# Output projection of a two-layer diffusion block: latent tiles kept in PSUM through both norms, and a planner that knows a shared port

## The chip, the cores and the metric

One core of a Trainium2 chip runs the whole program in one launch. Its engines are TensorE (PE, matmuls; PEld is its weight load), VectorE (DVE), ScalarE (ACT), GpSimd (POOL) and SyncE (SP, which issues most of the DMAs). The metric is the device time of one execution in microseconds, as the median of several runs.

## The reference

Two layers over 1024 latent tokens and 256 context tokens, 1024 channels, everything in float32. Each layer makes modulation vectors, projects the tokens, runs two kinds of attention and a convolution, and joins them in `o`. The part that matters here comes behind that, and then a mixture of 16 experts in which each expert takes its best tokens:

```python
x  = layer_norm(ALPHA * x + g1 * (o @ w_out[l]), ln1_g[l], ln1_b[l])   # ALPHA = sqrt(2)
h2 = layer_norm(x) * (1 + sc2) + sh2
aff = softmax(h2 @ w_router[l])                  # 16 experts
g, idx = top_k(aff.T, 128)                       # 128 latents (32 context tokens) for each expert
x  = layer_norm(ALPHA * x + g2 * scatter_add(experts(h2[idx]) * g), ln2_g[l], ln2_b[l])
```

The context tokens go the same way in layer 0 alone. In layer 1 only the latents do.

## The kernel before

Per layer, `p2` (with `p1`) projects, the attention follows, `p4` (line 1574) does the output projection, the two norms, the router and the search for the experts' tokens, and `moe` runs the experts. A float32 product is made of three matmuls on operands split into a high and a low part (`hi`, `lo`).

`p4` goes by tiles of 128 tokens: eight of latents, and in layer 0 two of context behind them. A tile's steps, with their lines:

1. Load the attention's output `ot` and the reciprocal sums `rb`, multiply them (L1700, on DVE for tiles 0 and 1, else on POOL), take the high part (L1710 on DVE, L1712 on ACT) and the low part (L1715, on DVE for latents, on POOL for context).
2. 48 matmuls in two halves of 512 columns (L1732 to L1734) into PSUM tiles `po` of one bank each; four are in rotation.
3. For latents, DVE multiplies each half by the gate row out of PSUM into an SBUF tile `t1` (L1742), which frees the bank, and adds the residual: `x*ALPHA + t1` (L1836). For context, ACT copies `po` to `t1` and POOL does the rest.
4. Statistics by halves (L1764), aggregation (L1770), epsilon (L1771), and the power -1/2 on POOL (L1774).
5. The first norm with its gain and shift (`lng`, `lnb`), by the tile's kind. Kind "d" (tiles 0 to 3): DVE makes -mean*rstd on one column (L1791), ACT normalizes (L1794), POOL multiplies by the gain (L1818), DVE adds the shift (L1820). Kind "h" (tiles 4 to 6) is the same in halves (L1807, L1810, L1813). Kind "f" (tile 7) is two DVE passes (L1785, L1788).
6. ACT scales the result by ALPHA into `ac` (L1844), which SP stores for the closing of the layer. Statistics again, and the second norm with the modulation rows, in the same kind.
7. SP stores the tile. PE transposes it (L1866), ACT copies that out (L1871), PE makes the logits (L1880), DVE the maximum (L1884), ACT the exponential (L1888), DVE the reciprocal and the division (L1891, L1892). PE transposes the affinities (L1901) and ACT keeps them in `aff` (L1905).

When all the latents' affinities are there, DVE searches: 16 rounds of MAX8, FIND_INDEX8 and MATCH_REPLACE8 (L1987 to L1990). The positions feed an indirect DMA (L2081) that fetches the tokens for `moe`.

The order of the work in `p4` is written by a planner, `Plan`: every operation has an engine, a price in us, operations that it needs, and slots that it takes (`t1=4, po=4, ...`). An engine that comes free takes the ready operation with the longest way to the end, and each engine's queue gets the operations in this order; at run time a queue is strictly in order. The planner knew the engines, not what two of them share:

```python
            return max(t, free.get(o["eng"], 0.0))          # Plan.run: when an operation can start
        ...
        P = Plan(ot=3, rb=3, x=2, oh=3, t1=4, po=4, tp=2, hT=1, lg=2, ac=1, raw=4, w=4)
        ...
    KINDS = [["dd"] * 4 + ["hh"] * 3 + ["ff", "dd", "ff"]] * 2
    GE, TE, LE = "pp", "pp", "pp"
```

The first weights of layer 1's experts are loaded while `p4` runs. Four of them are split there, `w_hi` on ACT (L2044) and `w_lo` on POOL (L2050). They are traced behind the plan, in a block of their own; a split gives its load's place free, and SP then loads another weight into it:

```python
            for c in range(self.PAIRS):
                self.w_hi(c)
                self.w_lo(l, c, nc.gpsimd)
                self.w_load(l, len(ring) + c)
```

Of the kernel before, what the change touches and what calls it, by code (L numbers as in the profile page):

```python
# [8 lines left out]
F32 = mybir.dt.float32  # L9
# [130 lines left out]
# ---------------------------------------------------------------- the kernel  # L140

class Plan:
    """Orders operations by a forecast: each has an engine, a price in us and the operations it needs. An engine that
    comes free takes the ready operation with the longest way to the end. A resource has n slots, taken in turn."""
# [11 lines left out]
    def op(self, eng, cost, f, after=(), new=(), use=(), lag=None, rank=0.0):  # L156
        o = dict(eng=eng, cost=cost, f=f, after=[x for x in after if x], new=list(new), 
                 lag=self.lags.get(eng, self.LAG) if lag is None else lag, own=lag is None or lag <= self.LAG,
                 rank=rank, n=len(self.ops), end=None)
        for h in (*new, *use):  # L160
            h["users"].append(o)
        self.ops.append(o)
        return o

    def run(self):
# [11 lines left out]
        def start(o):  # L177
# [9 lines left out]
            return max(t, free.get(o["eng"], 0.0))  # L187
        while ready:
# [16 lines left out]
class Kern:  # L205
# [5 lines left out]
    # -- small helpers  # L211
# [20 lines left out]
    def place(self, pool, shape, dt, *names):  # L232
        """Fixes the order of a pool's tiles in memory."""
# [6 lines left out]
    def split(self, hi, lo, src, hi_eng="act"):  # L240
        """src = hi + lo, hi of 12 bits."""
# [7 lines left out]
    def bcast_rows(self, src, n, parts=128):  # L249
        """A row of n values in DRAM, as an access pattern that repeats it over partitions."""  # L250
# [9 lines left out]
    # -- constants  # L260
# [96 lines left out]
    def adaln_col(self, w, junk, l, t, i):  # L357
        """Column t of a layer's modulation vectors, for x (0) or the context (1)."""
# [26 lines left out]
    def nrm(self, p, mv, n, tag):  # L385
        """(rstd, -mean * rstd), both [128, n]."""
# [4 lines left out]
    def ln_fast(self, x, mean, rs, g, b):  # L391
        """A norm with its affine map on the vector engine alone."""
# [4 lines left out]
    def ln_a(self, x, rs, nm, g):  # L397
        """A norm and its gain."""
# [4 lines left out]
    def p1(self, l, p, ps, vhi, vlo, W, prep_load, prep_split):  # L403
        """Closes the layer before (l > 0), first norm and modulation, values, the first projections."""
# [15 lines left out]
        # the values' weights  # L420
# [33 lines left out]
        for n, t in enumerate(tiles):  # L454
# [13 lines left out]
            if n == 2 and l > 0:  # L468
                ld.append(P.op("scatter", self.XS, lambda: None, after=ld[-1:]))  # the last scatter
# [88 lines left out]
        # transposed, modulated, in two parts  # L558
# [34 lines left out]
        # values  # L593
# [18 lines left out]
        # gates of the convolution, first tokens  # L612
# [48 lines left out]
    # -- projections  # L661

    def p2(self, l):
# [13 lines left out]
        # the lower part overlaps what the experts hold longest  # L677
# [24 lines left out]
        # the rest, channels on partitions  # L702
# [128 lines left out]
    # -- attention  # L831
# [21 lines left out]
    def early(self, l):  # L853
        """Masks, sinks and room for the first units of attention."""
# [19 lines left out]
    def early_units(self, l):  # L874
        """The row maxima of the first two units, as closures."""
# [9 lines left out]
    def keys(self, p, name, n, src):  # L885
        """Per head [k_hi; k_lo] and [k_hi; 1], keys along the free axis."""
# [25 lines left out]
    def su_load(self, u, srcs, part):  # L912
        """A unit's 1024 query columns: [hi; hi] and [lo; maximum]; srcs gives (columns, hi, lo)."""
# [24 lines left out]
    def su_rows(self, u, sink, dst):  # L938
        """The last row of the queries' second part, the negated maximum, and the sink's weights."""
# [112 lines left out]
    def make_units(self, l):  # L1052
# [4 lines left out]
        # 8 blocks of 128 queries: columns (kv head, head, query)  # L1057
# [22 lines left out]
        # heads over all queries of the grid  # L1080
# [37 lines left out]
        # the context's queries: kv head g, columns (head, query)  # L1118
# [75 lines left out]
    def recip(self, src, outs, w, sink=None):  # L1194
        """outs = 1 / (src + sink), runs of values in DRAM, w to a partition; two stages."""
# [71 lines left out]
    def conv_ln(self, P, l, un, after):  # L1267
        """The norm over a unit's channels, as operations."""
# [49 lines left out]
        # silu(y) = h (1 + tanh h), h = y / 2  # L1318
# [31 lines left out]
    def attention(self, l):  # L1350
# [140 lines left out]
        # the rest of the modulation, the output projection's weights  # L1491
# [18 lines left out]
        # the convolution  # L1510
# [21 lines left out]
        # the reciprocals of the denominators  # L1532
# [28 lines left out]
    # -- output projection, second modulation, routing  # L1561
# [12 lines left out]
    def p4(self, l):  # L1574
# [12 lines left out]
        # affinities: experts on partitions, the halves of the latents from 0 and 32, the context from 64  # L1587
# [916 lines left out]
```

## Time and profile before

| what | value |
|---|---|
| time, median of 3 runs | 2952.28 us (2948.66 to 2956.59) |
| profiled execution, span from first to last instruction | 2951.7 us; no time beside the span is recorded for it |
| PE busy | 2632.2 us, 89% |
| DVE busy | 2228.7 us, 76% |
| ACT busy | 1618.6 us, 55% |
| POOL busy | 949.7 us, 32% |
| mean granted clock of PE | 0.942 of full speed |

Busy time counts from an instruction's start to its end, so what an instruction waits for inside itself counts as busy. The `p4` stages lie at about 600 to 813 us (layer 0) and 2116 to 2315 us (layer 1) from the span's start.

### The profile page before, as it was taken

The page shows a single profiled execution, that of the slowest core. Times are in us where ns is not written, and L with a number is a line of the kernel's source. Part 1 is how long each engine was busy: PE and PEld are TensorE (multiplying, and loading weights), DVE is VectorE, ACT ScalarE, POOL GpSimd, SP SyncE. Part 2 cuts the span into 40 slices and gives each one's busy share as a digit, 9 for nine tenths or more (in the row PEclk, how much of TensorE's full clock was granted, in tenths as well). Part 3 has the DMA queues.
Part 4 walks back from the last instruction along what each step waited for, and adds up shares of the span by engine and source line. Part 5 has one row for each costly group of instructions (what it writes and reads, how often), then busy time and mean ns, then how long its engine had stood idle before and what let it go on. Part 6 is the DMA issues. An engine that isn't in the chain of part 4 may idle for free. (4 is left out here: it accounts for less than half of the span.)

```text
span 2951.7 us, 37404 instructions
## 1 busy us (share of the span) xinstructions
PE 2632.2 (89%) x13657; PEld 2070.0 (70%) x13657; DVE 2228.7 (76%) x3074; ACT 1618.6 (55%) x2045; POOL 949.7 (32%) x680
## 2 busy tenths in 40 slices
PE   7998988988589999999999499999986599999995
PEld 4986544566479898988888388655565477777774
DVE  6367598478869998888887835566588788888888
ACT  3224667623346665666666343687433377777774
POOL 2046687345412120201110516685054011111113
PEclk8999999989689999999999699999996799999998
DMA  6254744483458897979886414563453699999983
GB/s 244 74 181 148 202 136 108 115 245 120 188 211 314 309 335 285 336 292 327 301 319 226 149 54 157 172 184 104 138 183 151 235 372 373 372 374 372 373 341 135
DMA packets 204353, 682.86 MB, mean 231 GB/s; under 512 B 25637, under 2 KB 97630, under 8 KB 148870
## 3 DMA queue, kind: packets, MB, share of 16 engines
q1 hardware_dynamic: 191834, 641.23, 59.9%
q0 software_dynamic: 12336, 39.25, 5.3%
q8 instruction: 107, 1.75, 0.2%
q14 instruction: 76, 0.62, 0.1%
HBM read 600.45 MB, written 79.84 MB: 230 GB/s over the span
## 5 line engine op out<-in xcount | busy, mean ns | idle before, releaser
L2050 DVE TENSOR_TENSOR lo<-raw,hi 128x2048 fp32r<-128x2048 f32 x284 | 641.1, 2284 | 7.2 <-ACT hi L2044 7.1
L2044 ACT ACTIVATE hi<-raw 128x2048 fp32r<-128x2048 f32 x289 | 552.1, 1913 | 86.1 <-PE gu L2164 38.1
L2124 PE MATMUL gu<-xt,hi 128*128 128x320 f32 x2048 | 528.7, 332 | 0.9 <-DVE xt L2110 0.9
L2125 PE MATMUL gu<-xt,lo 128*128 128x192 f32 x2048 | 513.1, 251 | 0.0
L2240 POOL DMA_INDIRECT s_acc<-yo,i x31 | 76.3, 2462 | 1121.2 <-DVE yo L2238 1121.2
L1252 POOL TENSOR_TENSOR cy<-cy,csq 128x512 f32<-128x512 f32 (+1 forms) x300 | 386.1, 1302 | 109.2 <-ACT csq L1248 100.0
L2125 PEld LDWEIGHTS gu<-xt,lo 128*128 128x128 f32 x2048 | 392.4, 192 | 0.6
L2124 PEld LDWEIGHTS gu<-xt,hi 128*128 128x128 f32 x2048 | 385.6, 188 | 1.8 <-DVE xt L2110 1.1
L1178 PE MATMUL O<-P,v 128*65 128x512 f32 (+7 forms) x592 | 279.5, 561 | 12.9 <-ACT P L1171 12.6
L1248 ACT ACTIVATE csq<-ch,cw 128x512 f32<-128x512 f32 (+1 forms) x300 | 198.9, 673 | 46.9 <-POOL cy L1252 43.2
L2163 PE MATMUL gu<-hi,xt 128*128 128x512 f32 x512 | 204.5, 399 | 0.0
L2164 PE MATMUL gu<-hi,xt 128*128 128x512 f32 x512 | 202.8, 396 | 0.0
L2165 PE MATMUL gu<-lo,xt 128*128 128x512 f32 x512 | 202.8, 396 | 0.0
L730 PE MATMUL pj<-hhi,whi 128*128 128x512 f32 (+1 forms) x512 | 188.4, 368 | 9.1 <-ACT whi L244 9.1
L732 PE MATMUL pj<-hhi,wlo 128*128 128x512 f32 (+1 forms) x512 | 188.0, 367 | 1.1 <-DVE wlo L247 1.1
L731 PE MATMUL pj<-hlo,whi 128*128 128x512 f32 (+1 forms) x512 | 187.8, 367 | 0.0
L2050 DVE TENSOR_TENSOR lo<-more,hi 128x2048 fp32r<-128x2048 f32 x80 | 182.1, 2284 | 0.0
L2044 ACT ACTIVATE hi<-more 128x2048 fp32r<-128x2048 f32 x80 | 152.1, 1906 | 19.5 <-PE gu L2206 9.8
L1732 PE MATMUL po<-hi,ohi 128*128 128x512 f32 x288 | 123.0, 427 | 41.1 <-DVE ohi L1710 17.4
L361 DVE CUSTOM_DVE_ANT_0 adj<-adw,srow,bmod 128x1024 bf16<-128x1024 f32 x96 | 133.7, 1392 | 33.3 <-DMA adw<-in_wmt 31.6
L1171 ACT ACTIVATE P<-ST 128x512 f32<-128x512 f32 (+1 forms) x200 | 114.5, 580 | 51.8 <-PE ST L1154 28.2
L2132 ACT ACTIVATE t<-gu 128x320 f32<-128x320 f32 x128 | 55.4, 433 | 119.3 <-PE gu L2125 119.0
(318 smaller groups left out, 6004.2 us busy)
## 6 DMA issues: line engine op xcount, KB each, us to landing
raw<-in_wmoe SPq DMA_DIRECT2D x289, 1024.0 KB
more<-in_wmoe SPq DMA_DIRECT2D x80, 1024.0 KB
adw<-in_wmt SPq DMA_DIRECT2D x24, 1024.0 KB
srow<-in_wmoe SPq DMA_DIRECT2D x15, 1024.0 KB
wraw<-in_win SPq DMA_DIRECT2D x26, 512.0 KB
x<-in_x SPq DMA_DIRECT2D x16, 512.0 KB
adw<-in_wmt SPq DMA_DIRECT2D x16, 512.0 KB
q<-s_q SPq DMA_DIRECT2D x64, 128.0 KB
```

Source lines behind the costliest of these rows:

```text
L730: nc.tensor.matmul(o[:, :w], whi[:, k], hhi[:, k, sl], start=k == 0, stop=False)
L732: nc.tensor.matmul(o[:, :w], wlo[:, k], hhi[:, k, sl], start=False, stop=k == 7)
L1178: nc.tensor.matmul(o[:V1, o0:o0 + w], self.v[:, t["kt"], t["v"] * V1:t["v"] * V1 + V1], t["P"][:, :w], start=t["first"], stop=t["last"] is ...
L1248: nc.scalar.activation(z[:, :w], h, AF.Copy, scale=c)
L1252: nc.gpsimd.tensor_tensor(st["y"], st["y"], st.pop(("z", t))[:, :w], op=ALU.add)
L2044: self.nc.scalar.activation(h, self.S["raw", i], AF.Copy)
L2050: eng.tensor_tensor(lo, r, h.bitcast(F32), op=ALU.subtract)
L2124: nc.tensor.matmul(o[:, f, :320], hi[:, k, fs], xt[:, k], start=k == 0, stop=False)
L2125: nc.tensor.matmul(o[:, f, :192], lo[:, k, fs], xt[:, k, :192], start=False, stop=k == 7)
L2163: nc.tensor.matmul(o, xt[:, kk, 0], hi[:, k], start=kk == 0, stop=False)
L2164: nc.tensor.matmul(o, xt[:, kk, 1], hi[:, k], start=False, stop=False)
L2165: nc.tensor.matmul(o, xt[:, kk, 0], lo[:, k], start=False, stop=kk == 7)
```

## The change

The latents' tiles now stay in PSUM. One `po` tile holds both halves in two banks, and two such tiles are in rotation instead of four halves. Gate, sum, both norms and the statistics work in place on it (new function `affine_o`, two DVE passes per norm); only the second norm's shift writes `t1` in SBUF, in halves. The kinds "d" and "h" are gone for latents, and with them ACT's normalization and POOL's gain products. The low part `lo` of tiles 2 to 7 moves from DVE to POOL. Context tiles keep their way, but for -mean*rstd, which is a `tensor_scalar` now. The softmax division moves from DVE to ACT.

The plan gets a resource "port": every priced POOL operation, and each DVE operation marked with `port=True`, takes it, so that no two of these are planned at once. Several prices are changed. In layer 1, the four weight splits get an order in the queues: `w_hi` behind the last `keep` on ACT, `w_lo` behind the last `root` on POOL.

The diff, cut to its core (comments and docstrings, which the change also takes out, are left out here):

```diff
-    def __init__(self, slack=0.0, lags=None, **slots):
+    def __init__(self, slack=0.0, lags=None, ported=False, **slots):
+        self.ported = ported
...
-    def op(self, eng, cost, f, after=(), new=(), use=(), lag=None, rank=0.0):
+    def op(self, eng, cost, f, after=(), new=(), use=(), lag=None, rank=0.0, port=False):
+        port = self.ported and (port or eng == "pool" and lag is None and cost > 0)
...
-            return max(t, free.get(o["eng"], 0.0))
+            return max(t, free.get(o["eng"], 0.0), free.get("port", 0.0) if o["port"] else 0.0)
...
+            if o["port"]:
+                free["port"] = o["end"]
...
-        P = Plan(ot=3, rb=3, x=2, oh=3, t1=4, po=4, tp=2, hT=1, lg=2, ac=1, raw=4, w=4)
+        P = Plan(ported=True, ot=3, rb=3, x=2, oh=3, t1=4, po=2, tp=2, hT=1, lg=2, ac=1, raw=4, w=4)
...
-            pick = lambda s: po if ctx and s[i - 8] == "p" else ve
-            e, el, et = pick(self.GE), pick(self.LE), pick(self.TE)
+            el, et = po if i > 1 else ve, po if ctx and self.TE[i - 8] == "p" else ve
...
+            hp = P.new("po")
             for n in range(2):
-                hp = P.new("po")
...
-                        if k == 0:
-                            q["o", n] = self.rot(ps, [128, 512], F32, "po", 4)
-                        o, ns = q["o", n], slice(n * 512, n * 512 + 512)
+                        if n == 0 and k == 0:
+                            q["o"] = self.rot(ps, [128, 2, 512], F32, "po", 2)
+                        o, ns = q["o"][:, n], slice(n * 512, n * 512 + 512)
...
-                    o = P.op(pe, 1.29, mm, [parts[k], W[k], o], new=[hp] if k == 0 else [],
-                             use=[H["oh"], hw[k]] + ([hp] if k else []), rank=old)
+                    o = P.op(pe, 1.395, mm, [parts[k], W[k], o or first], new=[hp] if n == 0 and k == 0 else [],
+                             use=[H["oh"], hw[k]] + ([hp] if n or k else []), rank=old)
+                    first = first or o
...
+                def gate(q=q, n=n, cond=cond):
+                    nc.vector.tensor_tensor(q["o"][:, n], q["o"][:, n], rows[cond][0][:, n * 512:n * 512 + 512], op=ALU.mult)
...
+            hold = H["t1"] if ctx else hp
...
-                    nc.vector.bn_stats(q["st"][:, n, :], q["t1"][:, n * 512:n * 512 + 512])
+                    nc.vector.bn_stats(q["st"][:, n, :], q["t1"][:, n * 512:n * 512 + 512] if ctx else q["o"][:, n])
...
-                    nc.gpsimd.tensor_tensor(q["rs"], q["rs"], self.mhalf[:, :1], op=ALU.pow)
+                    ends_at[po] = nc.gpsimd.tensor_tensor(q["rs"], q["rs"], self.mhalf[:, :1], op=ALU.pow)
...
+            def affine_o(dep, g, b, uses, new=None, q=q):
+                two = lambda x: x.rearrange("p (a b) -> p a b", a=2)
+                def f1():
+                    nc.vector.scalar_tensor_tensor(q["o"], q["o"], q["mv"][:, 0, 0:1], two(g()), op0=ALU.subtract, op1=ALU.mult)
+                def f2():
+                    nc.vector.scalar_tensor_tensor(q["o"], q["o"], q["rs"], two(b()), op0=ALU.mult, op1=ALU.add)
+                def f3(n):
+                    if n == 0:
+                        q["t1"] = self.rot(p, [128, D], F32, "t1", 4)
+                    ns = slice(n * 512, n * 512 + 512)
+                    nc.vector.scalar_tensor_tensor(q["t1"][:, ns], q["o"][:, n], q["rs"], b()[:, ns], op0=ALU.mult, op1=ALU.add)
+                u = dict(use=[hp] + uses, rank=old)
+                o = P.op(ve, 1.28, f1, dep, **u)
+                if new is None:
+                    o = P.op(ve, 1.28, f2, [o], **u)
+                    return [o, o]
+                o1 = P.op(ve, 0.7, lambda: f3(0), [o], new=[new], **u)
+                return [o1, P.op(ve, 0.7, lambda: f3(1), [o1], use=u["use"] + [new], rank=old)]
...
-                    nc.vector.scalar_tensor_tensor(q["nm"], q["mv"][:, :, 0], -1.0, q["rs"], op0=ALU.mult, op1=ALU.mult)
+                    nc.vector.tensor_scalar(q["nm"], q["mv"][:, :, 0], q["rs"], -1.0, op0=ALU.mult, op1=ALU.mult)
...
-                        nc.vector.scalar_tensor_tensor(q["t1"][:, ns], q["x"][:, ns], ALPHA, q["t1"][:, ns],
+                        nc.vector.scalar_tensor_tensor(q["o"][:, n], q["x"][:, ns], ALPHA, q["o"][:, n],
                                                        op0=ALU.mult, op1=ALU.add)
...
-            o = affine([o, *ln], kinds[0], lambda: lng, lambda: lnb, [])
+            o = affine([o, *ln], kinds[0], lambda: lng, lambda: lnb, []) if ctx else \
+                affine_o([o, *ln], lambda: lng, lambda: lnb, [])
...
-                nc.scalar.activation(q["ac"], q["t1"], AF.Copy, scale=ALPHA)
+                nc.scalar.activation(q["ac"], q["t1"] if ctx else q["o"].rearrange("p a b -> p (a b)"), AF.Copy, scale=ALPHA)
...
                 nc.vector.reciprocal(q["sm"][:, 2:3], q["sm"][:, 1:2])
-                nc.vector.tensor_scalar(q["e"], q["e"], q["sm"][:, 2:3], None, op0=ALU.mult)
+            def share(q=q):
+                nc.scalar.activation(q["e"], q["e"], AF.Copy, scale=q["sm"][:, 2:3])
...
-                self.w_hi(c)
-                self.w_lo(l, c, nc.gpsimd)
+                with self.tc.issue_after(ends_at[ac].ins):
+                    self.w_hi(c)
+                with self.tc.issue_after(ends_at[po].ins):
+                    self.w_lo(l, c, nc.gpsimd)
...
-    KINDS = [["dd"] * 4 + ["hh"] * 3 + ["ff", "dd", "ff"]] * 2
-    GE, TE, LE = "pp", "pp", "pp"
+    KINDS = "dd", "ff"
+    TE = "pp"
```

## Rows read from the trace of the kernel before

**Rows 1.** Windows by stage: length, busy PE, PEld, DVE, ACT, POOL, clock, DMA.
```profile
830.00:1600.00 770.00, 770.00 (x5402) 671.98 (x5402) 656.82 (x709) 464.75 (x477) 118.51 (x58) 1.00 0.83 303
2120.00:2276.40 156.40, 127.84 (x576) 106.34 (x574) 129.41 (x175) 52.44 (x81) 77.21 (x45) 0.84 0.51 167
2276.40:2315.00 38.60, 0.54 (x2) 0.35 (x2) 36.23 (x87) 2.53 (x3) 4.50 (x1) 0.50 0.77 323
...
2330.00:2600.00 270.00, 263.63 (x1182) 212.16 (x1181) 232.80 (x147) 192.24 (x135) 32.72 (x14) 1.00 0.94 361
```

**Rows 2.** Groups by line, 2130 to 2330 us: count, busy us, mean ns, idle before.
```profile
L1836 DVE SCALAR_TENSOR_TENSOR t<-x,t 128x512 f32<-128x512 f32 x16 | 25.0, 1579 | 0.3
...
L1764 DVE BATCH_NORM_STATS2 p4st<-t 128x6 f32<-128x512 f32 x32 | 21.3, 684 | 0.3
L1791 DVE SCALAR_TENSOR_TENSOR p4nr<-mv,p4nr 128x1 f32<-128x1 f32 x14 | 19.1, 1361 | 5.5 <-POOL p4nr L1774 5.5
...
L1742 DVE TENSOR_TENSOR t<-po,raw 128x512 f32<-128x512 f32 x16 | 10.6, 682 | 2.9 <-PE po L1734 2.5 <-PE tp L1866 0.3
```

**Rows 3.** Timeline of DVE, both layers' stages: start us, length us, instruction.
```profile
629.26 0.69 DVE L1742 TENSOR_TENSOR t<-po,raw 128x512 f32<-128x512 f32 x1 [0.41 <-PE po L1734]
...
758.22 0.69 DVE L1987 MAX8 tv<-aff 48x8 f32<-48x512 f32 x1 [2.20 <-ACT aff L1905]
...
779.73 4.54 DVE L1785 SCALAR_TENSOR_TENSOR t<-t,mv,raw 128x1024 f32<-128x1024 f32 x1
...
2135.49 0.69 DVE L1742 TENSOR_TENSOR t<-po,raw 128x512 f32<-128x512 f32 x1 [2.53 <-PE po L1734]
...
2137.55 0.67 DVE L1742 TENSOR_TENSOR t<-po,raw 128x512 f32<-128x512 f32 x1
...
2228.64 0.21 DVE L1770 BATCH_NORM_AGGREGATE mv<-p4st 128x2 f32<-128x12 f32 x1
2228.88 0.15 DVE L1771 TENSOR_SCALAR p4nr<-mv 128x1 f32<-128x1 f32 x1
2229.76 4.44 DVE L1791 SCALAR_TENSOR_TENSOR p4nr<-mv,p4nr 128x1 f32<-128x1 f32 x1 [0.72 <-POOL p4nr L1774]
...
2246.75 1.28 DVE L1742 TENSOR_TENSOR t<-po,raw 128x512 f32<-128x512 f32 x2
...
2265.90 1.28 DVE L1788 SCALAR_TENSOR_TENSOR t<-t,p4nr,raw 128x1024 f32<-128x1024 f32 x1
...
2276.42 0.69 DVE L1987 MAX8 tv<-aff 48x8 f32<-48x512 f32 x1 [0.85 <-ACT aff L1905]
```

**Rows 4.** Timeline of POOL, both layers' stages.
```profile
698.73 2.91 POOL L1715 TENSOR_TENSOR olo<-ot,ohi 128x1024 fp32r<-128x1024 f32 x1
...
2229.70 4.49 POOL L2050 TENSOR_TENSOR lo<-raw,hi 128x2048 fp32r<-128x2048 f32 x1
```

**Rows 5.** Timeline of PE: logits in layer 0, last matmuls in layer 1.
```profile
693.88 1.85 PE L1880 MATMUL lg<-wr,hT 128*128 128x16 f32 x16
695.58 0.48 PE L1732 MATMUL po<-hi,ohi 128*128 128x512 f32 x1
...
2241.59 0.39 PE L1732 MATMUL po<-hi,ohi 128*128 128x512 f32 x1
2241.82 0.40 PE L1733 MATMUL po<-lo,ohi 128*128 128x512 f32 x1
2242.06 0.39 PE L1734 MATMUL po<-hi,olo 128*128 128x512 f32 x1
2242.29 1.04 PE L1866 MATMUL tp<-ident,t 128*128 128x128 f32 x8
```

**Rows 6.** Single lines: count, shortest, median and longest in ns.
```profile
L1836 DVE SCALAR_TENSOR_TENSOR t<-x,t x32: 677/1462/2593, 627.4 to 2248.6; 128x512 f32<-128x512 f32 x32
...
L1785 DVE SCALAR_TENSOR_TENSOR t<-t,mv,lng x3: 1268/1270/1271, 733.7 to 2253.7; 128x1024 f32<-128x1024 f32 x3
...
L1844 ACT ACTIVATE ac<-t x18: 1039/1056/1062, 646.5 to 2262.2; 128x1024 f32<-128x1024 f32 x18
```

More of the change, by code (lines that the diff above doesn't have):

```diff
@@ L154, in new @@
         return dict(name=name, users=[])
-    def op(self, eng, cost, f, after=(), new=(), use=(), lag=None, rank=0.0):
-        o = dict(eng=eng, cost=cost, f=f, after=[x for x in after if x], new=list(new),
+    def op(self, eng, cost, f, after=(), new=(), use=(), lag=None, rank=0.0, port=False):
+        port = self.ported and (port or eng == "pool" and lag is None and cost > 0)
+        o = dict(eng=eng, port=port, cost=cost, f=f, after=[x for x in after if x], new=list(new),
                  lag=self.lags.get(eng, self.LAG) if lag is None else lag, own=lag is None or lag <= self.LAG,
@@ L1629, in lo @@
                 nc.vector.tensor_tensor(wlo[c], raws[c], whi[c].bitcast(F32), op=ALU.subtract)
-            o = P.op(ac if c >= self.WD else ve, 1.8 if c >= self.WD else 1.13, hi, new=[hw[c]], use=[hr[c]], rank=self.WR[l] - self.WS[l] * c)
-            W.append(P.op(ve, 2.2, lo, [o], use=[hr[c]], rank=self.WR[l] - self.WS[l] * c))
+            o = P.op(ac if c >= self.WD else ve, 1.8 if c >= self.WD else 1.13, hi, new=[hw[c]], use=[hr[c]], rank=self.WR[l] - self.WS[l] * c,
+                     port=c < self.WD)
+            W.append(P.op(ve, 2.28, lo, [o], use=[hr[c]], rank=self.WR[l] - self.WS[l] * c, port=True))
         self.cnt["hi"] = self.cnt["lo"] = -1
@@ L1637, in p4 @@
         for parts, f, g in self.late:
-            o = P.op(ve, 0.3, g, [load(0.3, f, rank=-60.0 * min(parts))], lag=2.5)
+            o = P.op(ve, 0.3, g, [load(0.3, f, rank=-60.0 * min(parts))], lag=2.5, port=True)
             for x in parts:
@@ L1700, in den @@
                 (nc.vector if i < 2 else nc.gpsimd).tensor_tensor(q["ot"][:, 0:6], q["ot"][:, 0:6], q["rb"], op=ALU.mult)
[L1701 removed]
+            a = P.op(ve if i < 2 else po, 0.96 if i < 2 else 1.77, den, [a, b], use=[H["ot"], H["rb"]], rank=old, port=True)
             halves = [(0, 2), (2, 4), (4, 6), (6, 8)] if i < 2 else [(0, 8)]
@@ L1747, in out, with gate_c @@
                         q["t1"] = self.rot(p, [128, D], F32, "t1", 4)
-                    nc.scalar.activation(q["t1"][:, n * 512:n * 512 + 512], q["o", n], AF.Copy)
-                k = dict(new=[H["t1"]] if n == 0 else [], use=[hp] + ([H["t1"]] if n else []), rank=old)
-                if e == po:
-                    o = P.op(ac, 0.6, out, [o, *gated[-1:]], **k)
-                    k = dict(use=[H["t1"]], rank=old)
-                k["use"] = k["use"] + [hrow[cond][0]]
-                gated.append(P.op(e, 0.62 if e == ve else 1.24, gate, [o, lrow[cond][0], *gated[-1:]], **k))
+                    nc.scalar.activation(q["t1"][:, n * 512:n * 512 + 512], q["o"][:, n], AF.Copy)
+                def gate_c(q=q, n=n, cond=cond):
+                    ns = slice(n * 512, n * 512 + 512)
+                    nc.gpsimd.tensor_tensor(q["t1"][:, ns], q["t1"][:, ns], rows[cond][0][:, ns], op=ALU.mult)
+                if ctx:
+                    o = P.op(ac, 0.6, out, [o, *gated[-1:]], new=[H["t1"]] if n == 0 else [],
+                             use=[hp] + ([H["t1"]] if n else []), rank=old)
+                    gated.append(P.op(po, 1.24, gate_c, [o, lrow[cond][0], *gated[-1:]], use=[H["t1"], hrow[cond][0]], rank=old))
+                else:
+                    gated.append(P.op(ve, 0.68, gate, [o, lrow[cond][0], *gated[-1:]], use=[hp, hrow[cond][0]], rank=old))
             if ctx:
@@ L1828, in p4 @@
                 o = P.op(ac, 0.95, grow, [x], use=[H["x"]], rank=old)
-                o = P.op(et, tt[et], total, [o, *gated], use=[H["x"], H["t1"]], rank=old)
+                o = P.op(et, tt[et], total, [o, *gated], use=[H["x"], H["t1"]], rank=old, port=True)
                 o = [o, o]
```

64 lines of the change are left out of this document (23 added, 41 removed).

## Prediction

> **What bounds the kernel now.** I read the windows by stage first, then the groups by line inside the output-projection stage of each layer, then the timelines of VectorE (DVE), GpSimd (POOL) and TensorE (PE) there. In the expert stages PE is busy without a break (770.00 of 770.00 us in layer 0, 263.63 of 270.00 in a stretch of layer 1), so what begins earlier in front of them ends earlier by as much [rows 1]. In front of them lies the projection stage, then the search for each expert's tokens on DVE, during which PE works 0.54 us of 38.60 [rows 1]. The search cannot start before the last latent tile's affinities, so the date of its first MAX8 (2276.42 in layer 1, 758.22 in layer 0 [rows 3]) is what the change can move.
>
> In layer 1's stage DVE works 129.41 of 156.40 us, PE 127.84 [rows 1]. Much of DVE's share is waiting inside instructions. The sum with the residual takes 1579 ns in the mean [rows 2], at best 677 [rows 6]; the one-column product that makes -mean*rstd takes 1361 ns [rows 2], against 0.15 us for an epsilon, also one column [rows 3]. The gate, which reads PSUM and one SBUF row, has a mean of 682, and the statistics, one input, 684 [rows 2]. At 2229.76 the one-column product lasts 4.44 us, just while POOL splits a weight for 4.49 us [rows 3, 4]. So a DVE instruction with two SBUF inputs stands while POOL reads, and one with a single SBUF input does not. Of layer 1's stage that is 16*(1.58-0.68) = 14.4 us for the sums and 14*(1.36-0.15) = 16.9 us for the products, 31 us in two lines alone.
>
> **The change part by part.**
>
> *DVE per latent tile.* Two gates and two sums at 0.68, four statistics at 0.684 [rows 2], two aggregations at 0.21 and epsilons at 0.15 [rows 3], two subtract-and-gain passes at 1.27 [rows 6] and the first shift at 1.28 [rows 3], two half shifts at 0.68 like the gate, and 0.33 for maximum and reciprocal, one-column operations of the epsilon's size: 1.36 + 1.36 + 2.74 + 0.72 + 2.54 + 1.28 + 1.36 + 0.33 = 11.7 us. Each of these now has PSUM on one side or one input only, so none should stand for POOL. The price of a DVE write into PSUM no row shows. The nearest row, a PSUM read, costs 0.68, as much as the SBUF sum at its best [rows 2, 6]; I take that for both, and for the upper bound 0.1 more on each of ten half-tile writes, 1 us per tile. The Trainium skill's page "VectorE: DVE Perf Modes" (Rules for kernel authors) says the opposite of this design: accept the slow rate on a matmul output, or copy it to SBUF first if many operations follow. By the rows the copy would save nothing here: the float32 gate from PSUM and the SBUF sum cost the same, so the sum stays as it is by either.
>
> *PE per latent tile.* Forty-eight matmuls at (2242.29-2241.59)/3 = 0.233 us are 11.2 us; the logits take 695.58-693.88 = 1.7, the transposes at most 1.04 [rows 5]: 13.9 us. That is above DVE's 11.7, so PE is the floor of the period.
>
> *Two PSUM slots in place of early release.* Before, a bank came free after its gate. Now a tile keeps two banks until its second norm has been read, and only two tiles fit. The chain after a tile's second half: gate, sum and statistics 3*0.70, aggregation to epsilon 2228.88-2228.64 = 0.24, epsilon to the instruction behind POOL's root 2229.76-2228.88 = 0.88 [rows 3], gain and shift 2.6, second statistics 1.4 + 0.24 + 0.88, gain 1.3, two half shifts 1.4: 11.0 us. The scaled copy on ScalarE (ACT), 1.056 us [rows 6], now reads the same PSUM tile as the second statistics. If the two must not overlap, 1.2 us come on top; no row of before has two engines reading one PSUM tile. Between 11.0 and 12.2 I take 12.2. The Trainium skill's page "PSUM — Partial Sum Buffer" (PSUM bank collisions) says that two engines must not access one bank at once, reads included: by it the 12.2 holds, without it the sum below would lie 2.4 us per layer lower.
>
> With two slots a pair of tiles can't come round faster than 11.2 + 12.2, that is 11.7 us per tile: below PE's 13.9. So steady running is PE's, but the start loses its lead: the third tile, which now needs only freed gates, waits for the first tile's chain. That chain ends 12.2 us after the gate of its second half, at 629.26 + 12.2 = 641.5 in layer 0 and 2137.55 + 12.2 = 2149.8 in layer 1 [rows 3].
>
> *The low parts of tiles 2 to 7 move from DVE to POOL.* On POOL one takes 2.91 us [rows 4]. POOL loses the gain products, so it has room, but its queue is in order: a root behind a low part can wait up to 2.9 us, twice per tile. The planner's new port rule also shifts some low parts. From nothing to 5.8 us per tile; most of it meets the other tile's work. Together with dates that the planner misses I put 1.1 us on PE's floor: a period of 15.0. Now it is (2246.75-2135.49)/7 = 15.9 in layer 1 [rows 3].
>
> *Weight splits of the last layer.* Four splits on ACT and POOL leave the stage and follow its last affinity and last root. Four times 4.5 us on POOL [rows 4] lie under the 38.6 us of search [rows 1], so they cost nothing as long as their reloads, queued on SP behind the stage's last stores and other weight loads, come before the experts start; without that cover, up to 18 us. Their DVE stalls are already in the 31 us.
>
> *The tail.* From the end of the last shift, 2265.90 + 1.28, to MAX8 at 2276.42 there are 9.2 us [rows 3]. Transposes now begin with the first half (-0.6), the division moves to ACT (+0.2): 8.8. Behind the last matmul lie 12.2 + 8.8 = 21.0 us; now it is 2276.42 - 2242.45 = 34.0 [rows 3, 5].
>
> *Sum.* Tile 2 ends one matmul group after the first chain, tile 7 five periods later. Layer 1: 2149.8 + 11.2 + 75 + 21 = 2257.0, 19.4 us earlier. Layer 0: 641.5 + 11.2 + 75 + 21 = 748.7, 9.5 us earlier. In layer 0 a context pass stands 4.54 us instead of 1.27 at 779.73 [rows 3], while POOL splits; a plan that knows the port avoids that: 3.3. The context's other rows and the first-tile splits change by tenths. Total 32 us. The profiled span, 2951.7, lies 0.6 under the median of the runs, so the forecast is 2952.3 - 32 = 2920 us.
>
> **Rivals.** The period p decides: gain = 32 + 10*(15 - p), since five periods count in each layer.
> - *The floor holds exactly*, p = 13.9, and the chain is 11.0: 11 us and 2.4 per layer more than forecast, 48 us, 2904. For it: the plan's prices now fit what DVE does. Against: PE idles in front of gates in every stage now.
> - *Slots bite*: DVE's queue is in order, and a gate placed before a chain's end waits for PE while PE waits for that chain's slot. At p = 17 the gain is 12 us, 2940; it is zero at p = 18.2. Within 0.3% (9 us) means p from 17.3 to 19.1.
> - *Slower*: the same loop closed tightly, with PE starting a tile only when the one before it is nearly through; one slot in use would mean 11.2 + 12.2 = 23.4. At p = 20.5, half-way from 17 to that and beyond the 18.2 from which it decides, the loss is 23 us: 2975. For it: banks are held some 23 us instead of until the gate. Against: DVE's 11.7 leaves room in a 13.9 period.
> - *It does nothing*: the stalls go but other waits (the loads of tiles in layer 0, the reloads in layer 1) fill the place: 2952. Against: layer 1's stage shows no such wait now.
>
> **How the numbers follow.** Forecast (p from 14.2 to 16.5, gain 17 to 40) 0.57; floor or better 0.10; slots bite 0.18 (0.11 still faster, 0.06 within 0.3%, 0.01 slower); nothing 0.05; slower 0.10. A measurement of this kernel tells about 0.3% from no change. Faster by more: 0.57 + 0.10 + 0.11 = 0.78; within: 0.06 + 0.05 = 0.11; slower: 0.10 + 0.01 = 0.11. The range takes the forecast, the floor and most of the biting slots, and leaves out the slower case and the far end of better: 2902 to 2950.
>
> **What would show it.** Sums near 0.69 us and no product on one column for latents; the third tile's first matmul about 12 us after the first tile's second gate; gates of successive tiles 14 to 16 us apart; the last matmul some 21 us before MAX8; MAX8 near 749 in layer 0 and near 2244 in layer 1 (19 earlier, and 13 more from layer 0). The prediction is wrong if DVE waits long for PE inside chains, if the period is over 17, if POOL's roots wait for low parts, or if PE waits for weights after the search.

## The result, and the profile after

The changed kernel takes 2994.4 us (median of 4 runs, 2990.4 to 2998.1) against 2950.5 before: ratio 1.0145, 95% interval 1.0127 to 1.0164, so 44 us slower where 2920 was forecast. The profiled execution has a span of 2996.3 us.

Windows by stage of the changed kernel, with the columns of [rows 1]: the first expert stage, the last layer's projection up to its first MAX8, and the search.

```profile
860.00:1630.00 770.00, 770.00 (x5400) 671.99 (x5400) 657.14 (x710) 465.29 (x477) 118.57 (x58) 1.00 0.83 304
2152.00:2321.40 169.40, 126.22 (x577) 102.30 (x575) 101.55 (x165) 31.32 (x67) 34.12 (x28) 0.81 0.47 155
2321.40:2360.00 38.60, 0.56 (x2) 0.35 (x2) 36.24 (x87) 7.90 (x6) 17.94 (x4) 0.50 0.76 320
```

The expert stage and the search are as long as before. In the projection stage, both times taken from some 4 us behind its first matmul, DVE works 102 us instead of 129, and yet the stage grew from 156.4 to 169.4 us: both engines wait longer, PE 43 us of it instead of 29, DVE 68 instead of 27. Groups by line of DVE in that stage answer to [rows 2].

```profile
L1772 DVE BATCH_NORM_STATS2 p4st<-po 128x6 f32<-128x512 f32 x32 | 21.7, 692 | 7.5 <-PE po L1739 5.3 <-ACT ac L1860 1.6
L1804 DVE SCALAR_TENSOR_TENSOR t<-po,p4nr,raw 128x512 f32<-128x512 f32 x16 | 11.6, 743 | 0.4 <-POOL p4nr L1782 0.3
L1745 DVE TENSOR_TENSOR po<-po,raw 128x512 f32<-128x512 f32 x16 | 11.2, 699 | 45.2 <-PE po L1739 44.9
L1851 DVE SCALAR_TENSOR_TENSOR po<-x,po 128x512 f32<-128x512 f32 x16 | 11.1, 696 | 0.6
```

The sum (L1851) went from 1579 to 696 ns and the one-column product is gone: the stalls vanished. In their place DVE stands 45.2 us in front of gates (L1745), for PE; before it was 2.9 [rows 2]. The timeline of DVE shows one pair of tiles, and that of PE what it did meanwhile.

```profile
2207.80 0.70 DVE L1745 TENSOR_TENSOR po<-po,raw 128x512 f32<-128x512 f32 x1 [9.53 <-PE po L1739]
...
2211.72 0.70 DVE L1745 TENSOR_TENSOR po<-po,raw 128x512 f32<-128x512 f32 x1
...
2217.96 0.70 DVE L1745 TENSOR_TENSOR po<-po,raw 128x512 f32<-128x512 f32 x1 [3.64 <-PE po L1739]
...
2219.30 1.28 DVE L1795 SCALAR_TENSOR_TENSOR po<-po,mv,lng 128x1024 f32<-128x1024 f32 x1
2220.49 0.69 DVE L1745 TENSOR_TENSOR po<-po,raw 128x512 f32<-128x512 f32 x1
...
2233.28 0.74 DVE L1804 SCALAR_TENSOR_TENSOR t<-po,p4nr,raw 128x512 f32<-128x512 f32 x1
...
2235.41 1.41 DVE L1804 SCALAR_TENSOR_TENSOR t<-po,p4nr,raw 128x512 f32<-128x512 f32 x2
```

```profile
2193.68 0.77 PE L1737 MATMUL po<-hi,ohi 128*128 128x512 f32 x1
...
2217.53 0.39 PE L1739 MATMUL po<-hi,olo 128*128 128x512 f32 x1
...
2232.27 0.38 PE L1919 MATMUL lg<-ident,e 128*16 128x128 f32 x1 [9.08 <-ACT e L1910]
2233.21 1.09 PE L1882 MATMUL tp<-ident,t 128*128 128x128 f32 x4 [0.56 <-DVE mv L1778]
2234.08 0.79 PE L1737 MATMUL po<-hi,ohi 128*128 128x512 f32 x1
2234.67 0.63 PE L1738 MATMUL po<-lo,ohi 128*128 128x512 f32 x1
2235.10 0.63 PE L1739 MATMUL po<-hi,olo 128*128 128x512 f32 x1
...
2271.52 0.79 PE L1737 MATMUL po<-hi,ohi 128*128 128x512 f32 x1
```

The first tile's second gate is at 2211.72, but the first pass of its norm (2219.30) stands in the queue behind the second tile's gate, which waits for PE until 2217.96. From there DVE works both chains through each other. The first tile's last shift ends at 2234.02, 22.3 us after its second gate; the second tile's at 2236.82. In the next pair two passes go ahead of that gate, and the first tile's chain still takes 19.1 us (2252.40 to 2271.46). PE has nothing but small work from 2217.9 until a slot is free, takes its next matmul at 2234.08, and then does two tiles at a stretch, the first few matmuls 0.43 us apart instead of 0.23. The pairs before and after begin at 2193.68 and 2271.52: 40.4 and 37.4 us for two tiles, 19.5 each. In layer 0 the pairs behind the first begin at 653.85, 687.74 and 725.29, 17.9 us a tile.

Dates in us from the span's start, each the first instruction of its kind in the layer's stage (the first expert matmul is a transpose of the fetched tokens). "Chain order", "Ranks", "Parts" and "Best" are experiments below.

| | before | after | Ranks | Chain order | Parts | Best |
|---|---|---|---|---|---|---|
| layer 0: first MAX8 | 758.2 | 780.4 | 748.4 | 741.5 | 748.1 | 741.9 |
| layer 0: first expert matmul | 818.6 | 848.6 | 816.3 | 814.1 | 810.0 | 805.9 |
| layer 1: first projection matmul | 2115.9 | 2148.4 | 2115.2 | 2109.5 | 2110.0 | 2104.6 |
| layer 1: first MAX8 | 2276.4 | 2321.4 | 2263.8 | 2255.3 | 2253.6 | 2236.9 |
| layer 1: first expert matmul | 2319.7 | 2364.8 | 2307.1 | 2298.5 | 2297.0 | 2280.2 |

At the last line the changed kernel is 45.1 us late: 22.2 at layer 0's first MAX8, 7.8 more up to its experts, where the context tiles end the stage, 2.5 on the way to layer 1, and 12.6 there.

### The profile page after: what moved, and what is told of

It is laid out like the page before. It is cut to its first block, busy times and chain, and to the rows that moved or that the text cites. A ratio compares the mean times of both kernels' runs of the same rounds, so it can differ in the third digit from the quotient of the medians.

```text
span 2996.3 us, 37302 instructions
## 1 busy us (share of the span) xinstructions
PE 2632.8 (88%) x13657; PEld 2066.0 (69%) x13657; DVE 2186.5 (73%) x3048; ACT 1588.1 (53%) x2023; POOL 886.2 (30%) x652
## 4 chain that ended last, share of the span: by engine, by line
PE 58%; DVE 7%; DMA 3%; issue 2%; ACT 1%; POOL 1%; SPq 0%; DVEq 0%; POOLq 0%; ACTq 0%
PE gu L2145 12%; PE gu L2146 6%; PE gu L2184 4%; PE gu L2185 4%; PE gu L2186 4%; PE O L1183 3%; PE gu L2226 2%; PE gu L2217 2%; PE gu L2240 2%; PE gu L2227 2%; PE gu L2228 2%; PE gu L2241 2%; PE gu L2239 2%; PE pj L736 1%; PE pj L737 1%
## 5 line engine op out<-in xcount | busy, mean ns | idle before, releaser
L2065 ACT ACTIVATE hi<-more 128x2048 fp32r<-128x2048 f32 x80 | 152.1, 1906 | 19.5 <-issue 10.0
L1739 PE MATMUL po<-hi,olo 128*128 128x512 f32 x288 | 119.2, 414 | 3.4 <-DVE olo L1720 2.6
```

Of the source, the lines that this page charges most:

```text
L2065: self.nc.scalar.activation(h, self.S["raw", i], AF.Copy)
```

## The experiments

All ratios are to the kernel before, with 95% intervals; where two runs are compared "by the ratios", it is the difference of theirs times 2950 us. The question was which of three things keeps the slots: the order of the queues (A), the number of slots and the time that they are held (B), or a wait between the two halves of a tile (C).

### The order

**TensorE tile by tile** (e2_half_order). Each half's first matmuls depend on those of the half before, over all tiles:

```
-        routed, ends_at = [], {}
+        routed, ends_at, prev = [], {}, None
...
-            gated, first = [], None
+            gated, first = [], prev
...
-                    first = first or o
+                    first = prev = o
```

> The changed kernel with one thing different: TensorE takes the matmuls of the latent tiles strictly tile by tile and half by half (48, then the next tile's 48), where its plan laid two tiles through each other and ended both nearly together. Theory A, the order: with two slots that end 11 us apart, the chain of one tile (12 us) lies beside the matmuls of the other, and a tile comes round in about 14 to 15 us instead of 18 to 20; over the 8 latent tiles of each of the two layers that takes back about 27 us each, so about 2940 us. Theory B, the holding time: a slot is held for the matmuls and the whole chain whatever the order, so TensorE waits the same in sum and the time stays within 10 us of 2994.

Measured: 3014.9 us, 1.0222 (1.0206 to 1.0237). Both forecasts missed: stricter order on PE alone made it worse. DVE still had the second tile's gates inside the first tile's chain, and waited there for PE, here between the first tile's second pass and its second statistics (2250.55):

```profile
2244.29 1.29 DVE L1798 SCALAR_TENSOR_TENSOR po<-po,p4nr,lnb 128x1024 f32<-128x1024 f32 x1
2247.36 0.70 DVE L1745 TENSOR_TENSOR po<-po,raw 128x512 f32<-128x512 f32 x1 [1.77 <-PE po L1739]
2249.82 0.70 DVE L1851 SCALAR_TENSOR_TENSOR po<-x,po 128x512 f32<-128x512 f32 x1 [1.76 <-PE po L1739]
```

PE's timeline in this kernel brought theory C:

```profile
2171.68 0.50 PE L1737 MATMUL po<-hi,ohi 128*128 128x512 f32 x1 [1.52 <-DVE po L1851]
...
2174.13 0.50 PE L1737 MATMUL po<-hi,ohi 128*128 128x512 f32 x1 [0.79 <-DVE p4st L1772]
```

These are matmuls on a tile's second half, which wait for DVE's sum and statistics on its first half. The halves lie in different banks, but are one PSUM tile of the program.

**DVE chain after chain** (e16_chain_order). One dependency is added, nothing of PE's ranks is touched:

```
-        routed, ends_at = [], {}
+        routed, ends_at, chain = [], {}, []
...
-                    gated.append(P.op(ve, 0.68, gate, [o, lrow[cond][0], *gated[-1:]], use=[hp, hrow[cond][0]], rank=old))
+                    gated.append(P.op(ve, 0.68, gate, [o, lrow[cond][0], *gated[-1:], *chain], use=[hp, hrow[cond][0]], rank=old))
...
             done = o
+            chain = [] if ctx else o[1:]
```

> The changed kernel with one dependency more: a latent tile's gate waits for the end of the chain of the latent tile ahead of it, so that VectorE takes chain after chain; ranks as in the change (3 apart), TensorE's order as the plan then makes it. If VectorE's order is the cause, a tile again comes round in about 14 us and most of the 56 us that the ranks gave are there: 2935 to 2952 (the plan still leaves transposes and logits in clumps). If TensorE's order was needed too: 2965 or more.

Measured: 2933.7 us, 0.9953 (0.9937 to 0.9969), by the ratios 57 us below the changed kernel and 1 us better than forecast. DVE's timeline has the first gates of six tiles in a row 13.0 to 13.6 us apart, with no wait in front; two of them:

```profile
2176.30 0.69 DVE L1745 TENSOR_TENSOR po<-po,raw 128x512 f32<-128x512 f32 x1
...
2189.32 0.69 DVE L1745 TENSOR_TENSOR po<-po,raw 128x512 f32<-128x512 f32 x1
```

So with two slots held to the end, PE's order alone did harm, while DVE's, with PE as the plan then lays it (also tile by tile), takes the whole loss away. DVE's order with PE's tiles still in pairs was not tried. Two slots do for a chain that isn't interrupted.

**Ranks 12 us apart** (e10_rank12), which orders both queues: `old = -3.0 * i` becomes `old = -12.0 * i`.

> The changed kernel with one number different: the plan ranks each tile 12 us behind the one ahead of it instead of 3. Its queues then take tile after tile: VectorE ends a tile's chain before it takes the next tile's gate (where it laid two chains through each other), and TensorE starts the first pair of matmuls of each tile when the slot two tiles back is free. Theory A', the joint order of VectorE and TensorE makes two slots too few: slots now come free 12 to 14 us apart, a tile comes round in 14 to 16 us instead of 18 to 20, and the time falls to 2925 to 2945. Theory B, holding a slot through matmuls and chain is too long in any order: 2980 or more, as the strict order of TensorE alone (3015) showed.

Measured: 2938.3 us, 0.9969 (0.9957 to 0.9981). First gates of four tiles in a row, from DVE's timeline:

```profile
2172.85 0.70 DVE L1745 TENSOR_TENSOR po<-po,raw 128x512 f32<-128x512 f32 x1 [4.17 <-PE po L1739]
...
2186.78 0.70 DVE L1745 TENSOR_TENSOR po<-po,raw 128x512 f32<-128x512 f32 x1 [0.79 <-PE po L1739]
...
2200.69 0.70 DVE L1745 TENSOR_TENSOR po<-po,raw 128x512 f32<-128x512 f32 x1 [0.77 <-PE po L1739]
...
2214.60 0.70 DVE L1745 TENSOR_TENSOR po<-po,raw 128x512 f32<-128x512 f32 x1 [0.77 <-PE po L1739]
```

The period is 13.9 us, the floor of PE that the prediction worked out; the last two tiles come 14.6 us apart.

**The same number on the kernel before** (e13_before_rank12).

> The kernel before with one number different: ranks 12 us apart instead of 3, the number that took 56 us off the changed kernel. If the number mends what the change brought (two chains through each other on two slots held to their end), the kernel before, which copies out of PSUM at once, has nothing to mend: 2942 to 2952. If closer order is worth something in any dataflow (a shorter tail, fewer tiles open), 2930 to 2940, and the gain of the changed kernel with it is not to be set against the kernel before alone.

Measured: 2950.3 us, 1.0002 (0.9992 to 1.0012). The ranks mend what the change brought; by themselves they do nothing for the kernel before.

### The slots

**Three slots** (e6_three_slots): `po=3, tp=1, lg=1` instead of `po=2, tp=2, lg=2`.

> The changed kernel with a third pair of PSUM banks for the latent tiles (the transposes and the logits keep one bank each instead of two); all work on the latent tiles stays in place in PSUM. Theory A, the order alone: the plan, asked for the same priorities, still lays tiles through each other; 2980 or more. Theory B, two slots are too few for a chain of 12 us behind matmuls of 11: the third slot lets TensorE go on while two chains run, a tile comes round in about 14 to 15 us, and the time falls to 2925 to 2945. If the single banks of transposes and logits bite instead, their waits for ScalarE show at the transposes' line and the time stays near 2970.

Measured: 2953.2 us, 1.0024 (1.0012 to 1.0037): by the ratios 36 of the 43 us lost are back without a word on order, but the kernel stays 7 us slower than before. The time lies between the forecasts: in the last layer's stage PE waits 4.1 us in front of transposes for ACT, as the third of them had it, but not enough for 2970.

**Early release** (e5_early_release). The first pass of the first norm writes to SBUF, and what follows works there:

```
-  nc.vector.scalar_tensor_tensor(q["o"], q["o"], q["mv"][:, 0, 0:1], two(g()), ...)
+  q["t1"] = self.rot(p, [128, D], F32, "t1", 4)
+  nc.vector.scalar_tensor_tensor(two(q["t1"]), q["o"], q["mv"][:, 0, 0:1], two(g()), ...)
```

> The changed kernel with the slot given back early: the first pass of the first norm of a latent tile writes to SBUF, and the rest of the chain (second pass, second statistics, second norm) works there, its passes planned as users of the port; gate, sum and first statistics stay in PSUM, the order of the plan is its own. Theory A, the order alone: the plan still lays pairs of tiles through each other, so at most a third of the 44 us comes back, 2980 us or more. Theory B, the holding time: the slot is free about 4 us after its last matmul instead of 12, TensorE is no longer held, and the time falls to about 2930 us plus what the second passes lose to POOL (16 passes of some 1 to 2 us each, 15 to 30 us, if they meet it): 2930 to 2960.

Measured: 2936.1 us, 0.9955 (0.9938 to 0.9972). Order or a slot held for less undo the loss, one slot more undoes most of it: the loop needs all three, tiles in pairs, two slots, held to the end of the chain.

### The halves

**A PSUM tile for each half** (e8_two_tiles); passes over 1024 columns become two over 512:

```
-  if n == 0 and k == 0:
-      q["o"] = self.rot(ps, [128, 2, 512], F32, "po", 2)
+  if k == 0:
+      q["o", n] = self.rot(ps, [128, 512], F32, f"po{n}", 2)
```

> The changed kernel with the two halves of a latent tile in two PSUM tiles of the program instead of one (same banks, same two slots; passes over 1024 columns become two over 512). In the trace of the strict order TensorE waited 1.5 us for VectorE's sum on one half before it went on with the other half, and VectorE waited 1.75 us for TensorE's other half. Theory C, these mutual waits of the two halves are the loss: they go, and the time falls to 2940 to 2960. Theory B, the chain as a whole holds the slot: the pairs stay in step, the tile's period stays 18 to 20 us and the time stays within 12 us of 2994.

Measured: 2979.9 us, 1.0111 (1.0093 to 1.0129): by the ratios 10 us better than the change, far from C and at the edge of B (2982). A second cause, not the first: in layer 1 the pairs' first gates come at 2195.14, 2232.84 and 2269.11, 18.5 us a tile instead of 19.5.

**With the ranks** (e11_rank12_two_tiles).

> Both edits together: ranks 12 us apart and a PSUM tile for each half. Theory A' alone: the same as the ranks alone, or up to 3 us slower by the shorter passes (0.12 us more for each of 16 pairs of passes in each layer). Theory C on top: another 5 to 10 us faster than the ranks alone, since a half's gate no longer waits for the other half's matmuls. Theory B: 2980 or more.

Measured: 2929.0 us, 0.9939 (0.9918 to 0.9960), 9 below the ranks alone, as C on top had it.

### The other parts by themselves

**The splits alone, on the kernel before** (e3_splits_only): `self.w_hi(c)` under `issue_after(ends_at[ac].ins)`, `self.w_lo(...)` under `issue_after(ends_at[po].ins)`.

> The kernel before, with one part of the change alone: the second layer's first splits of the expert weights are issued behind the last router step of ScalarE and the last root of POOL. Theory A, these splits were in the way: the three waits of VectorE behind the 4.4 us splits in the second layer's latent tiles go, and the time falls by 9 to 13 us, to about 2940. Theory B, they were hidden, or what is put off is then missed by the experts' first matmuls: within 5 us of 2950.

Measured: 2935.7 us, 0.9953 (0.9940 to 0.9967), 11 us below the median of the kernel before measured beside it and 14 by the ratio: the splits were in the way, theory A. **The port-aware plan alone** (e4_port_only): the plan, its flags and costs, on the kernel before. The edit also makes -mean*rstd a `tensor_scalar`, as in the change; the expectation doesn't name that.

> The kernel before with the plan's knowledge of the shared port alone: passes with two SBUF inputs and POOL's operations are laid beside each other no more, and the costs are those of the changed kernel; data stay in SBUF, splits and ranks as before. If the waits of the passes behind POOL (1.58 us for 0.7 us of work at the sum) are what the plan can lay apart, up to 16 x 0.9 us of them go in each layer, and where TensorE isn't already the bound some 5 to 10 us of it show: 2937 to 2945. If the port kept free only moves the waiting into the queues: 2947 to 2960.

Measured: 2933.6 us, 0.9945 (0.9929 to 0.9962), 16 us, more than forecast. How much of it is the plan's and how much the `tensor_scalar`'s no run separates. **Both, without the work in PSUM** (e17_port_and_splits; "Parts" in the table).

> The kernel before with both other parts of the change, the plan's knowledge of the port and the splits behind the last root, and without the work in PSUM. If the two gains (16 and 11 us) come from different waits they add up: 2920 to 2926. If the port-aware plan had already laid the passes clear of the 4.4 us splits, the sum is that of the plan alone: 2930 to 2936. Against the best version with PSUM (2912) this says what the work in PSUM is worth.

Measured: 2924.8 us, 0.9913 (0.9894 to 0.9931). 24 us below the median beside it and 26 by the ratio: within the interval the two gains add up. The two lines that [rows 2] charged with 31 us, in groups by line of DVE from 2100 to 2270 us, first with the splits moved, then with the plan alone, then with both:

```profile
L1836 DVE SCALAR_TENSOR_TENSOR t<-x,t 128x512 f32<-128x512 f32 x16 | 22.9, 1453 | 0.3
L1791 DVE SCALAR_TENSOR_TENSOR p4nr<-mv,p4nr 128x1 f32<-128x1 f32 x14 | 4.4, 314 | 7.8 <-POOL p4nr L1774 7.8
```

```profile
L1840 DVE SCALAR_TENSOR_TENSOR t<-x,t 128x512 f32<-128x512 f32 x16 | 17.8, 1111 | 0.2
L1795 DVE TENSOR_SCALAR p4nr<-mv,p4nr 128x1 f32<-128x1 f32 x14 | 2.9, 208 | 11.8 <-POOL p4nr L1778 11.6
```

```profile
L1840 DVE SCALAR_TENSOR_TENSOR t<-x,t 128x512 f32<-128x512 f32 x16 | 11.3, 705 | 0.2
```

Moving the splits takes the product from 1361 to 314 ns, the other form with the plan takes it to 208; the plan and the splits together bring the sum to 705, its price in PSUM being 696. Nearly all the waiting in these two lines goes without PSUM. **The same with the ranks** (e18_port_splits_rank12).

> The same with ranks 12 us apart. In the run with the port-aware plan alone TensorE ended its matmuls in the second layer at 2210.8 but the first MAX8 came 44 us later, with transposes and logits of several tiles in between; closer ranks should bring them forward: 2910 to 2920, as good as the best with PSUM. If order is worth nothing where PSUM is left at once, as in the kernel before with the ranks alone (2950): the same as without the ranks, within 4 us.

Measured: 2946.9 us, 0.9993 (0.9983 to 1.0004), 22 us worse than without the ranks on the same chip; both forecasts missed. The number isn't good in itself. In the last layer's stage DVE now waits 14.6 us for POOL's gain products in front of the shifts (L1824), 3.0 without the ranks; no run tests whether that is the cause. **The ranks without the moved splits** (e14_rank12_no_splits).

> The changed kernel with ranks 12 us apart, and the second layer's first weight splits issued as in the kernel before (not behind the last root and the last router step). My prediction put the move of the splits at nothing in the new dataflow, since passes in PSUM don't wait for POOL: 2938 plus or minus 4. If the splits stand in POOL's queue ahead of the roots of the latent tiles, as 4.4 us pieces, each adds a wait of up to 4 us to a chain that now sets the period: 2943 to 2955.

Measured: 2943.7 us, 0.9978 (0.9964 to 0.9991) against 0.9969 with them moved: at the lower end of the second forecast by the median, but only 3 us by the ratios, and the intervals overlap, so it stays open whether there is a loss.

### Toward the best

**Early release with the ranks** (e12_early_rank12).

> The changed kernel with the early release of the slot (first pass of the first norm to SBUF) and ranks 12 us apart. If what is left above TensorE's 13.9 us a tile in the run with the early release alone is the clump of transposes and logits behind the last matmul (29 us), the spread order takes some 8 us of it in the second layer, and in the first layer as far as the context tiles let it: 2922 to 2932. If order no longer matters once the slots come free early: 2936 plus or minus 4.

Measured: 2930.0 us, 0.9943 (0.9927 to 0.9960), as the first forecast had it. **And a PSUM tile for each half** (e15_early_rank12_two; "Best" in the table).

> Three edits to the changed kernel together: the slot given back after the first pass, ranks 12 us apart, a PSUM tile for each half. What is left in the run with ranks and two tiles is a start (TensorE idle 14 us in each layer until the first chain ends) and a tail of 18 us. With the early release the start shortens to about 5 us, and the passes in SBUF meet POOL again: 2918 to 2928 if the start sets the end of the layer; 2927 to 2933 if what is saved there is lost to the passes or to the context tiles.

Measured: 2912.3 us, 0.9874 (0.9852 to 0.9896), faster than both kernels, better than either forecast, and some 12 us below the two other parts without PSUM. What it gained beyond the forecast has no run of its own.

## Why the prediction was wrong

**What held.** *DVE per latent tile*, 11.7 us: the lines of the changed kernel's stage sum to 94.7 us for eight tiles, 11.8 each (a gate in place 0.699, a sum 0.696, a half shift 0.743). *PE per latent tile*, 13.9: so in the run with the ranks. It is a floor only where transposes and logits keep pace: with the chain order, 13.4 us a tile, more of them are left for the end (27.1 us from the last matmul to MAX8, against 20.0). *The tail*: 21.0 forecast, 2263.8 - 2243.8 = 20.0 in the run with the ranks, 25.3 in layer 1 of the changed kernel.

The chain itself came to 10.95 us with the ranks, where 12.2 was taken:

```profile
2188.97 0.70 DVE L1745 TENSOR_TENSOR po<-po,raw 128x512 f32<-128x512 f32 x1
...
2196.08 0.70 DVE L1772 BATCH_NORM_STATS2 p4st<-po 128x6 f32<-128x512 f32 x1 [1.09 <-ACT ac L1860]
...
2198.51 1.41 DVE L1804 SCALAR_TENSOR_TENSOR t<-po,p4nr,raw 128x512 f32<-128x512 f32 x2
```

The wait for ACT that the 1.2 stood for is there, 1.09 us: the last statistics begin just after ACT's copy of the same tile (2195.02, 1.03 us long). By the Trainium skill's page "PSUM — Partial Sum Buffer" (PSUM bank collisions) two engines must not read one bank at once. The trace shows the two kept apart; no run let them meet. What came out shorter are the two waits of 0.88 us for POOL's root: the first pass of each norm needs only the mean, and begins 0.15 and 0.07 us after its epsilon has begun (2191.41 and 2197.06). That the sum lies near the 11.0 is luck.

**The step that failed** is in *Two PSUM slots in place of early release*: "a pair of tiles can't come round faster than 11.2 + 12.2, that is 11.7 us per tile: below PE's 13.9. So steady running is PE's". 23.4 us per pair is what two tiles need when one's chain lies beside the other's matmuls. That is a matter of order, and I took it from the engines' capacity. The plan ranks tiles only 3 us apart and otherwise by the longest way, so it laid two tiles' matmuls and then their chains through each other. Then nothing lies beside anything: 24 us of matmuls, then 13 to 16 of chains with PE held, 37 to 40 us a pair. The rival *Slots bite* names the place (a gate ahead of a chain's end in DVE's queue), and *Slower* the result, with 19.5 us a tile near its 20.5 (half-way from 17 to 23.4 would be 20.2); what I set against the latter, that DVE's 11.7 leaves room in 13.9, is about capacity again.

The formula gives 2957 for 17.9 us a tile in layer 0 and 19.5 in layer 1; 37 us are not in it. The traces show where they lie:
- *The start.* The third tile's first matmul came at 653.85 where 641.5 was forecast, and in layer 1, whose stage began 32.5 us late, at 2193.68 instead of 2182.3: 12 and 11 us late. The first tile's chain, with the second tile's laid through it, took 25.3 and 21.2 us from its second gate; in layer 0 7.3 of them are a wait for the load of the second tile's residual.
- *The tail.* From the last latent matmul to MAX8 went 30.5 us in layer 0 and 25.3 in layer 1, not 21.0.
- *The context tiles.* From MAX8 to the experts of layer 0 went 68.2 us instead of 60.4, where 3.3 were to be gained.
- *Against that*, the formula counts some 10 us too much, since the last two tiles end their matmuls together.

The mutual waits of the halves, 10 us by the run with two tiles, lie in the period (18.5 us there).

**Terms that were mis-sized even with the order mended** (with the ranks 9 us gained by the ratio, 12.6 at the table's last line, not 32):
- *Sum, layer 0*, 9.5 + 3.3. The first MAX8 came at 748.4 where 748.7 was forecast, but the experts only 2.3 us earlier. From MAX8 to the experts, where the context tiles end the stage, it is 67.9 us, 60.4 before. That "a plan that knows the port avoids" the 4.54 us context pass is refuted: the changed kernel has one of 4.87 (at 811.54), and with the ranks DVE's timeline has two while POOL does two weight splits in a row.

```profile
775.65 4.87 DVE L1816 SCALAR_TENSOR_TENSOR t<-t,mv,raw 128x1024 f32<-128x1024 f32 x1
780.63 5.33 DVE L1819 SCALAR_TENSOR_TENSOR t<-t,p4nr,raw 128x1024 f32<-128x1024 f32 x1
```

```profile
774.95 9.93 POOL L2071 TENSOR_TENSOR lo<-raw,hi 128x2048 fp32r<-128x2048 f32 x2
```

- *Sum, layer 1*: the third tile's first matmul, forecast for 2149.8 (12.8 earlier with layer 0's gain), came at 2158.07. The first chain, with the second tile's gates in it and 3.40 us of waiting for ACT, took 17.4 us from its second gate at 2139.70.
- *Weight splits*: the move was taken to cost nothing and its gain to be part of the 31 us of stalls. It costs nothing that a run shows (with the ranks the difference stays open), but on the kernel before it gains 11 to 14 us by itself, so the stalls in the two lines of [rows 2] had a cheaper cure than PSUM.
- *The low parts on POOL*, together with dates that the planner misses: 1.1 us a tile taken. With the ranks three of the five periods show none of it and the last two 0.7, when no low part is left on POOL. The second passes wait 1.7 us in that whole stage for a root. The low parts alone were not tried.

## What to carry to other kernels

A stage with few buffers can be bounded by the order in which in-order queues give them back, and not by the sum of work per engine: before trusting a rate, write down two rounds of each queue and see whether the holders of the buffers end together. When a buffer is to be held longer, look at what separates the holders in time (a priority, a dependency), or give it back early. Before moving data to escape a wait, try to move the work that is waited for: here the splits, the plan and the other form of the product gained 26 us by themselves, where the best version gained 37.

## What the runs showed of the hardware

- A float32 DVE operation that writes PSUM in place costs hardly more than one that leaves it: 699 against 682 ns for the gate over 128x512.
- The sum with one input in SBUF and one in PSUM did not stand for POOL: all 32 in the changed kernel took 695 or 696 ns, that at 2212.46 too, which lies inside a 2.4 us subtraction of POOL (2211.93). With both inputs in SBUF it took up to 2593 ns before [rows 6].
- By the Trainium skill's page "VectorE: DVE Perf Modes" (Rules for kernel authors) one accepts the slow rate on a matmul's output or copies it to SBUF first if many operations follow. Measured, each with the best order tried for it: out with the gate 2924.8, in place to the end 2929.0, out with the first pass of the norm, after gate, sum and statistics in place, 2912.3. The intervals of the first two overlap, and the three differ in more than this (the engines of the norms, the ranks), so no run here shows the page right or wrong.
- PE came back from its waits at the lower of its two clock levels: in the changed kernel the granted clock was 0.50 (1.2 GHz) from 2234.1 to 2237.2 us, behind the wait, with matmuls 0.43 us apart, and 1.00 (2.4 GHz) from 2238 to 2249, with 0.23. Over the stage it is 0.81, against 0.84 before [rows 1] and 0.94 in the best version.
